# A causal mask moved from matrix products to the row maximum, and partial-array products put side by side

## The chip, the cores and the metric

The kernel runs on one core of a Trainium2 chip. Four engines matter here. TensorE multiplies matrices, VectorE (DVE) and ScalarE (ACT) do element work, and SyncE (SP) issues the transfers from the chip's main memory; GpSimd (POOL) computes a few reciprocal square roots. Each engine works through its own queue in order, and waits where an instruction needs something from another engine or from an earlier instruction of its own. The metric is the time of one execution on the device, in microseconds (us).

## The reference

One decoder layer on 256 positions of width 1024. What the change touches is the first of three stages, the block attention; with 256 positions there is one key block, so it is plain causal attention over eight heads of width 64.

```python
def moba_attention(q, k, v):          # 8 heads of 64, one block of 256 keys
    s = jnp.einsum('bhqd,bhkd->bhqk', q, k) * 64 ** -0.5
    s = jnp.where(k_pos[None, :] <= q_pos[:, None], s, NEG_INF)   # causal mask, NEG_INF = -1e30
    p = jax.nn.softmax(s, axis=-1)
    return jnp.einsum('bhqk,bhkd->bhqd', p, v)

proj = rms_norm(x, g_pre_mix) @ w_in  # q, k, v of the attention; q, k, v, gate of the retention
mo = merge_heads(moba_attention(rotary(q), rotary(k), v))
ro = silu(rg) * rms_norm(retention(rotary(rq), rotary(rk), rv))
x = x + rms_norm(jnp.concatenate([mo, ro], -1) @ w_out, g_post_mix)
# then cross-attention (4 heads of 256) into 256 memory rows, then a SwiGLU feed-forward layer
```

The two lines on `s` are condensed here from the reference's code for gathered blocks.

## The kernel before, in words

All weights come in 130 blocks of 128 x 1024 floats. A block is split into a high part (ScalarE copies it to the matrix format, line 135) and a low part (VectorE subtracts, line 136), and each full product is made of three matrix products: high by high, high by low, low by high (lines 856 to 858, and 871 and 874 in the stages that hold the weights still). TensorE runs these full products almost without end; each of lines 856 to 858 covers the whole 128 x 128 array and streams 512 columns.

Between them stand small pieces of work, which are generators that the main loop resumes: a `yield n` puts the next piece n steps later, and the table `WAIT` holds these numbers by name. So the table, and the order in which pieces are spawned, set every engine's queue when the program is built; nothing is decided at run time. A split of a block is put in when no small piece was resumed in a step, or when blocks run low.

The 256 positions are two tiles of 128, t = 0 and t = 1. The names in the profile are these:

- `c_q`, `c_k`, `c_r`: four transposes each (`moba_qk`, line 216, and `ret_qk`, line 325); ScalarE copies the results to `qv` and `kr` (lines 217, 326, 327), from which the score products read.
- `s_m`: scores of the attention (line 275). A head has 64 rows, so a product uses half of the array's rows, and the two halves work as a pair. There are three units: m00 is tile 0 with eight heads of 128 keys; m10 and m11 are tile 1, four heads each of 256 keys. Each unit has two banks of scores and runs through `softmax_unit`: row maximum (line 231), negated and scaled (`nb`, line 235), exponentials with row sums (line 241), reciprocal and product with it (lines 244, 246), eight transposes (`pt_m`, line 254), and their copies `ptT` (ScalarE line 259, VectorE line 261).
- `maskb`, `identb`: the causal mask is added as a matrix product of the identity with the mask into the same bank (line 278), two per unit.
- `rs`, `ra`: scores of the retention (line 339, again 64 rows each) and their product with the decay table on VectorE (line 346); `ro` is the retention's output (lines 357, 360).
- `o_m`: the value products of the attention (line 304), which use 64 of the array's columns; tile 0 and tile 1 each have a stretch.
- `hl` is a split block, `R_mem` a copied row of norms, `rv` and `mv` copied projections, `junk<-memn` the mean squares of the memory rows.

The banks that `accS` hands out are four, used in turn: a new user waits until the engine that read the last one is done with it.

Of the kernel before, what the change touches and what calls it, by code (L numbers as in the profile page):

```python
# [7 lines left out]
F32 = mybir.dt.float32  # L8
F32R = mybir.dt.float32r
BF16 = mybir.dt.bfloat16  # L10
# [12 lines left out]
NQ = 130  # L23

WAIT = {
# [8 lines left out]
}  # L34
WARM = 8

# [6 lines left out]
def tile_hybrid_layer(  # L43
# [39 lines left out]
    def accS(name):  # L83
        return psS.tile([P, 512], F32, tag="S", name=name)
# [8 lines left out]
    xg = cpool.tile([P, 288], F32, tag="xg", name="xg")  # L93
    gp = xg[:, 0:32].rearrange("p (g k) -> p g k", g=4)
    x_sb = cpool.tile([P, 2, D], F32, tag="x", name="x_sb")
    identb = cpool.tile([P, P], BF16, tag="identb", name="identb")
    maskb = cpool.tile([P, P], BF16, tag="maskb", name="maskb")
    junk = cpool.tile([P, D], BF16, tag="junk", name="junk")
    mhalf = cpool.tile([P, 8], F32, tag="mhalf", name="mhalf")
    ident = cst[:, C_ID:C_ID + P]  # L100
# [116 lines left out]
        nc.scalar.activation(T[f"{kind}T"][:, :, tok(t)], c, AF.Copy)  # L217
        emitted.add(f"{kind}{t}")

    def softmax_unit(key, n, keys, scale, fill, row=None, finish=None):  # L220

        hn = n // 2
        s = [accS(f"s_{key}{b}") for b in range(2)]
        yield from fill(s)
        mx = small(f"mx_{key}")
        nb = small(f"nb_{key}")
        sums = small(f"sum_{key}")
        rs = small(f"rs_{key}")
        p = p4.tile([P, D], F32, tag="p4", name=f"p_{key}")
        for b in range(2):  # L230
            nc.vector.reduce_max(out=mx[:, b * hn:(b + 1) * hn], in_=s[b].rearrange("p (h k) -> p h k", h=hn),
                                 axis=AX.X)
        if row is None:
            esc = scale
            nc.vector.tensor_scalar(nb[:, :n], mx[:, :n], -scale, None, op0=ALU.mult)
        else:
            esc = rs[:, 7:8]
            nc.vector.tensor_scalar(esc, row[:, 0:1], scale, None, op0=ALU.mult)
            nc.vector.tensor_scalar(nb[:, :n], mx[:, :n], row[:, 0:1], -scale, op0=ALU.mult, op1=ALU.mult)
        for i in range(n):  # L240
            nc.scalar.activation(p[:, i * keys:(i + 1) * keys], s[i // hn][:, (i % hn) * keys:(i % hn + 1) * keys],
                                 AF.Exp, bias=nb[:, i:i + 1], scale=esc, accum_out=sums[:, i:i + 1])
# [3 lines left out]
        nc.vector.tensor_tensor(out=p3, in0=p3, in1=rs[:, :n, None].to_broadcast([P, n, keys]), op=ALU.mult)  # L246
        yield WAIT[f"nm_{key}"]
        if finish is None:
            pt = pt4.tile([P, 8, P], F32, tag="pt4", name=f"ptT_{key}")
            T[f"pt_{key}"] = pt  # L250
        for b in range(2):
            s2 = accS(f"pt_{key}{b}")
            for j in range(4):
                nc.tensor.transpose(s2[:, j * P:(j + 1) * P], p[:, (4 * b + j) * P:(4 * b + j + 1) * P], ident)  # L254
            src = s2.rearrange("p (j k) -> p j k", j=4)
            if finish is not None:
                finish(b, src)
            elif b == 0:
                nc.scalar.activation(pt[:, 0:4, :], src, AF.Copy)
            else:  # L260
                nc.vector.tensor_copy(pt[:, 4:8, :], src)

    def moba_unit(t, g):
        keys = P * (t + 1)
        n = D // keys
        hn = n // 2

        def fill(s):

            need(f"q{t}", *[f"k{u}" for u in range(t + 1)])  # L270
            for i in range(hn):
                j = g * hn + i
                for e in range(2):
                    rows = slice(64 * e, 64 * e + 64)
                    nc.tensor.matmul(s[e][:, i * keys:(i + 1) * keys], T["qT"][rows, j, tok(t)],  # L275
                                     T["kT"][rows, j, 0:keys], start=(i == 0), stop=False, skip_group_check=True)
            for e in range(2):
                nc.tensor.matmul(s[e].rearrange("p (h k) -> p h k", h=hn)[:, :, keys - P:keys], identb,
                                 maskb[:, None, :].to_broadcast([P, hn, P]), start=False, stop=True,
                                 skip_group_check=True)  # L280
            yield 0

        return softmax_unit(f"m{t}{g}", n, keys, 0.125, fill)

    def moba_units():
        yield from moba_unit(0, 0)
        yield WAIT["u1"]
        yield from moba_unit(1, 0)
        yield WAIT["u2"]
        yield from moba_unit(1, 1)  # L290

    def moba_pv(t):
        need("mv0", f"mv{t}")
        v = T["mv"]
        c = accC(f"o_m{t}")
        for j in range(4):
            for kb in range(t + 1):
                for e in range(2):
                    h = 2 * j + e
                    if t == 0:  # L300
                        rhs = T["pt_m00"][:, 4 * e + j, :]
                    else:
                        rhs = T[f"pt_m1{j // 2}"][:, 2 * (2 * e + j % 2) + kb, :]
                    nc.tensor.matmul(c[64 * e:64 * e + 64, j, :], v[:, kb, h * 64:h * 64 + 64], rhs,  # L304
                                     start=(kb == 0), stop=(kb == t), skip_group_check=True)
        split4("mixT", 0, t, c)
        yield 0


# [142 lines left out]
        return [pt4.tile([P, 4, 256], F32R, tag="pt4", name=f"{name}{i}") for i in range(2)]  # L452

    def cross_unit(t):
        def fill(s):
            qh, ql, kh, kl = T["cqh"], T["cql"], T["ckh"], T["ckl"]
            for h in range(4):
                for kk in range(2):
                    k = 2 * h + kk
                    tri(s[h // 2][:, (h % 2) * 256:(h % 2 + 1) * 256],  # L460
                        (qh[:, k, tok(t)], ql[k // 4][:, k % 4, tok(t)]), (kh[:, k, :], kl[:, k, :]), kk == 0, kk == 1)
                if h == 1:
                    yield WAIT[f"sc_c{t}"]
            emitted.add(f"cs{t}")
# [9 lines left out]
        return softmax_unit(f"c{t}", 4, 256, 0.0625, fill, rstd[f"x1{t}"], finish)  # L474

    def cross_pv(hp):
        need(f"pc0{hp}", f"pc1{hp}")
# [59 lines left out]
    def in_done(chunk, t, acc):  # L537
        if chunk == 0:
            spawn(moba_qk("q", t, acc), WAIT["mq"])
        elif chunk == 1:  # L540
            spawn(moba_qk("k", t, acc))
            if t == 1:
                spawn(moba_units(), WAIT["u0"])
        elif chunk == 2:
            spawn(ret_qk(t, acc))
            if t == 1:
                spawn(ret_scores(), WAIT["rsc"])
        elif chunk == 3:
            evac(T["rv"][:, t, :], acc, rstd[f"x{t}"][:, 0:1])
            emitted.add(f"rv{t}")  # L550
            if t == 1:
                spawn(ret_out(0), WAIT["ro0"])
                spawn(ret_out(1), WAIT["ro1"])
        elif chunk == 4:
            spawn(ret_gate(t, acc))
        else:
            evac(T["mv"][:, t, :], acc, rstd[f"x{t}"][:, 0:1])
            emitted.add(f"mv{t}")
            spawn(moba_pv(t), WAIT[f"pv{t}"])

    def out_done(c, t, acc):
        post_half("mix", t, c, acc)
# [214 lines left out]
        yield 0  # L777

    def x_stats():
        nc.vector.tensor_copy(identb, ident)  # L780
        nc.vector.tensor_copy(maskb, cst[:, C_MASK:C_MASK + P])
        for t in range(2):
            ss = small(f"ss_x{t}")
            mean_square(ss[:, 0:1], x_sb[:, t, :], D)
# [233 lines left out]
```

## Time and profile before

| what | value |
|---|---|
| median of 3 runs | 408.96 us (408.43 to 409.5) |
| the profiled execution: time, span | 409.01 us, 407.2 us |
| granted TensorE clock, mean | 0.996 |
| TensorE busy | 399.3 us (98% of the span) |
| VectorE busy | 283.2 us (70%) |
| ScalarE busy | 238.4 us (59%) |
| read from main memory | 74.76 MB, 186 GB/s over the span |

The span runs from the first to the last instruction on the core; the execution's own time is 1.8 us longer. In a timeline row the first number is the start, the second the duration, then come engine, line and operation, the tile written and the tiles read, the shapes, and the count of instructions merged; a bracket at the end gives idle time before the row and what ended it. A product of plain 32-bit operands stands as two instructions. Products overlap their ends, so the distance from one start to the next is what a product costs TensorE, not its duration; the same holds for VectorE and ScalarE in a lesser degree.

### The profile page before, as it was taken

What the parts mean: (1) busy time and instruction counts of PE and PEld (TensorE: products, weight loads), DVE (VectorE), ACT (ScalarE), POOL (GpSimd) and SP (SyncE); (2) the same over time, 40 slices, a digit from 0 to 9 for tenths busy, and PEclk for the clock granted to TensorE, in tenths of its full rate; (3) what the DMA queues carried; (4) which work ended last, traced back from release to release, by engine and by line L of the source; (5) the groups of instructions that cost most, each with busy time, mean ns of one, the idle gap of its engine ahead of it and who ended that gap; (6) DMA issues with size and microseconds to landing.
All of it is one profiled execution on the core that took longest, in us unless ns stands there. A gap on an engine that the chain in (4) does not pass through costs nothing.

```text
span 407.2 us, 5752 instructions
## 1 busy us (share of the span) xinstructions
PE 399.3 (98%) x2114; PEld 336.4 (83%) x2114; DVE 283.2 (70%) x456; ACT 238.4 (59%) x438; POOL 11.9 (3%) x21
## 2 busy tenths in 40 slices
PE   8999999999999999999999999999999999999993
PEld 4888787888888889888888888888888888888882
DVE  4885975765989966578359567794884685776632
ACT  5887785935776764686248566564563663564411
POOL 0010100100010000000010100000000000000000
PEclk9999999999999999999999999999999999999998
DMA  7998654475656566147206765675466468355001
GB/s 278 412 358 264 227 200 155 151 260 173 204 194 205 173 206 190 34 175 258 105 8 205 266 233 168 183 221 215 155 192 225 156 172 291 109 159 199 0 29 74
DMA packets 21627, 76.17 MB, mean 187 GB/s; under 512 B 2400, under 2 KB 2656, under 8 KB 21600
## 3 DMA queue, kind: packets, MB, share of 16 engines
q1 hardware_dynamic: 21456, 75.56, 55.2%
q8 instruction: 16, 0.26, 0.3%
q10 hardware_dynamic: 144, 0.26, 0.2%
q14 instruction: 11, 0.09, 0.1%
HBM read 74.76 MB, written 1.05 MB: 186 GB/s over the span
## 4 chain that ended last, share of the span: by engine, by line
PE 95%; issue 2%; DMA 1%; ACT 1%; DVE 0%; SPq 0%; DVEq 0%; POOLq 0%; POOL 0%
PE acc L871 23%; PE acc L874 12%; PE acc L856 12%; PE acc L858 12%; PE acc L857 12%; PE down L892 4%; PE down L893 4%; PE down L894 4%; PE acc L843 2%; DMA xr<-in_gx_dram 1%; PE s_m L275 1%; PE o_m L304 1%; PE pt_m L254 1%; PE ro L357 0%; PE s_c L444 0%
## 5 line engine op out<-in xcount | busy, mean ns | idle before, releaser
L136 DVE TENSOR_TENSOR hl<-raw,hl 128x1024 fp32r<-128x1024 f32 (+1 forms) x132 | 154.6, 1197 | 38.7 <-ACT hl L135 38.2
L135 ACT ACTIVATE hl<-raw 128x1024 fp32r<-128x1024 f32 (+1 forms) x132 | 132.9, 1037 | 9.4 <-DMA raw<-in_weights_dram 7.0
L871 PE MATMUL acc<-x2T,hl 128*128 128x512 f32 x288 | 72.5, 392 | 0.0
L871 PEld LDWEIGHTS acc<-x2T,hl 128*128 128x128 f32 x288 | 52.0, 189 | 9.4
L874 PEld LDWEIGHTS acc<-x2T,hl 128*128 128x128 f32 x288 | 39.3, 190 | 2.8
L874 PE MATMUL acc<-x2T,hl 128*128 128x256 f32 x288 | 40.1, 282 | 0.0
L892 PE MATMUL down<-hl,fT 128*128 128x512 f32 x88 | 34.3, 390 | 0.0
L893 PE MATMUL down<-hl,fT 128*128 128x512 f32 x88 | 34.3, 390 | 0.0
L894 PE MATMUL down<-hl,fT 128*128 128x512 f32 x88 | 34.2, 389 | 0.0
L856 PE MATMUL acc<-hl,xT 128*128 128x512 f32 x80 | 32.7, 409 | 0.0
L858 PE MATMUL acc<-hl,xT 128*128 128x512 f32 x80 | 31.3, 391 | 0.0
L857 PE MATMUL acc<-hl,xT 128*128 128x512 f32 x80 | 31.2, 390 | 0.0
L516 ACT ACTIVATE sg<-sg 128x256 f32<-128x256 f32 x18 | 7.5, 417 | 21.3 <-DVE sg L514 21.3
L894 PEld LDWEIGHTS down<-hl,fT 128*128 128x128 f32 x88 | 16.5, 188 | 3.5
L892 PEld LDWEIGHTS down<-hl,fT 128*128 128x128 f32 x88 | 16.5, 188 | 3.3
L893 PEld LDWEIGHTS down<-hl,fT 128*128 128x128 f32 x88 | 16.5, 188 | 3.3
L511 ACT ACTIVATE sg<-acc 128x256 f32<-128x256 f32 x18 | 6.8, 378 | 19.3 <-PE acc L874 19.2
L858 PEld LDWEIGHTS acc<-hl,xT 128*128 128x128 f32 x80 | 15.0, 188 | 3.3
L856 PEld LDWEIGHTS acc<-hl,xT 128*128 128x128 f32 x80 | 15.1, 188 | 3.1 <-issue 0.3
L447 ACT ACTIVATE fT<-sg 128x256 fp32r<-128x256 f32 x18 | 7.5, 419 | 17.0 <-DVE sg L528 16.9
L857 PEld LDWEIGHTS acc<-hl,xT 128*128 128x128 f32 x80 | 15.1, 188 | 2.7
L513 DVE TENSOR_TENSOR sg<-acc,sg 128x256 f32<-128x256 f32 x18 | 7.6, 421 | 12.7 <-ACT sg L511 12.7
(209 smaller groups left out, 695.0 us busy)
## 6 DMA issues: line engine op xcount, KB each, us to landing
raw<-in_weights_dram SPq DMA_DIRECT2D x129, 512.0 KB, 4.4
gpost<-in_gpost_dram SPq DMA_DIRECT2D x3, 512.0 KB, 5.6
x_sb<-in_x_dram SPq DMA_DIRECT2D x2, 512.0 KB, 6.9
memn<-in_mem_dram SPq DMA_DIRECT2D x2, 512.0 KB, 6.7
mr<-in_memT_dram SPq DMA_DIRECT2D x2, 512.0 KB, 5.3
out_dram<-x_sb SPq DMA_DIRECT2D x4, 256.0 KB, 2.0
xr<-in_gx_dram SPq DMA_DIRECT2D x1, 512.0 KB, 8.3
cst<-in_consts_dram SPq DMA_DIRECT2D x1, 512.0 KB, 7.9
```

The lines of the kernel that those rows point to most:

```text
L135: nc.scalar.activation(h[:, 0, n], raw[:, n], AF.Copy)
L136: nc.vector.tensor_tensor(out=h[:, 1, n], in0=raw[:, n], in1=h[:, 0, n].bitcast(F32), op=ALU.subtract)
L513: nc.vector.tensor_tensor(out=sg, in0=acc[:, 0:256], in1=sg, op=ALU.add)
L843: nc.tensor.matmul(accs[(c, t)], T["xT"][:, hx, 2 * kp + kk, tok(t)], h[:, hw, :], start=begin, stop=False)
L856: nc.tensor.matmul(acc, xh, h[:, 0, kk, :], start=(first and kk == 0), stop=False)
L857: nc.tensor.matmul(acc, xh, h[:, 1, kk, :], start=False, stop=False)
L858: nc.tensor.matmul(acc, xl, h[:, 0, kk, :], start=False, stop=(last and kk == 1))
L871: nc.tensor.matmul(acc, hls[q][:, 0, k * P:(k + 1) * P], T[f"{st}_k"][:, k, :], start=(k == 0), stop=False, skip_group_check=True)
L874: nc.tensor.matmul(acc[:, 0:256], hls[q][:, 1, k * P:(k + 1) * P], T[st][:, 0, k, :], start=False, stop=(k == 7), skip_group_check=True)
L892: nc.tensor.matmul(acc, fh, wh, start=first, stop=False, skip_group_check=True)
L893: nc.tensor.matmul(acc, fh, wl, start=False, stop=False, skip_group_check=True)
L894: nc.tensor.matmul(acc, fl, wh, start=False, stop=last, skip_group_check=True)
```

## The change

The mask is no longer a matrix product. VectorE adds it with an instruction that adds two operands, writes the sum back into the score bank and keeps the row maximum (`tensor_tensor_reduce`), one per head; the maximum over both heads' banks (`reduce_max`) stays for the cross-attention. A table of 256 columns, zeros and then the mask, takes the place of the two 16-bit tiles.

The score products of m00 and m10 are issued together, and those of m11 directly ahead of the first retention scores, instead of each with its own unit. The value products of both tiles are issued together, into two of the four score banks instead of the single bank that `accC` hands out. The table of waits is another one in nearly every entry, and two names are new: a wait after the maximum (`mx_`) and one halfway through the exponentials (`eh_`).

```diff
 WAIT = {
-    "cpb0": 1, "cpb1": 0, "cpv0": 7, "cpv1": 3, "cu0": 1, "cu1": 4, "ex_c0": 0, "ex_c1": 1, "ex_m00": 0,
+    "cpb0": 1, "cpb1": 3, "cpv0": 7, "cpv1": 1, "cu0": 0, "cu1": 2, "eh_c0": 2, "eh_c1": 1, "eh_m00": 2,
...
-    identb = cpool.tile([P, P], BF16, tag="identb", name="identb")
-    maskb = cpool.tile([P, P], BF16, tag="maskb", name="maskb")
+    maskz = cpool.tile([P, 256], F32, tag="maskz", name="maskz")
...
-    def softmax_unit(key, n, keys, scale, fill, row=None, finish=None):
+    def softmax_unit(key, n, keys, scale, s, row=None, finish=None):
...
-        for b in range(2):
-            nc.vector.reduce_max(out=mx[:, b * hn:(b + 1) * hn], in_=s[b].rearrange("p (h k) -> p h k", h=hn),
-                                 axis=AX.X)
+        if row is None:
+
+            for i in range(n):
+                a = s[i // hn][:, (i % hn) * keys:(i % hn + 1) * keys]
+                nc.vector.tensor_tensor_reduce(out=a, in0=a, in1=maskz[:, 256 - keys:256], scale=1.0, scalar=-3.0e38,
+                                               op0=ALU.add, op1=ALU.max, accum_out=mx[:, i:i + 1])
+        else:
...
+        yield WAIT[f"mx_{key}"]
         for i in range(n):
+            if 2 * i == n:
+                yield WAIT[f"eh_{key}"]
...
-            for e in range(2):
-                nc.tensor.matmul(s[e].rearrange("p (h k) -> p h k", h=hn)[:, :, keys - P:keys], identb,
-                                 maskb[:, None, :].to_broadcast([P, hn, P]), start=False, stop=True,
-                                 skip_group_check=True)
...
     def moba_units():
-        yield from moba_unit(0, 0)
+
+        units = [moba_scores(0, 0), moba_scores(1, 0)]
+        spawn(units[0])
         yield WAIT["u1"]
-        yield from moba_unit(1, 0)
+        spawn(units[1])
         yield WAIT["u2"]
-        yield from moba_unit(1, 1)
+        last = moba_scores(1, 1)
+        scores = ret_scores()
+        wait = next(scores)
+        spawn(scores, wait)
+        yield from last
...
-    def moba_pv(t):
-        need("mv0", f"mv{t}")
+    def moba_pv():
+        need("mv0", "mv1")
         v = T["mv"]
-        c = accC(f"o_m{t}")
...
+        banks = [accS("o_m0").rearrange("p (j m) -> p j m", j=4), accS("o_m1").rearrange("p (j m) -> p j m", j=4)]
+        for t in range(2):
+            c = banks[t]
```

The built queues differ in many places; three of them are shown, names with the program's buffer numbers. First VectorE, from the scores of m00 to the product with the reciprocal, before:

```order
L231 TENSOR_REDUCE mx_m_423<-s_m_411 128x4
L231 TENSOR_REDUCE mx_m_423<-s_m_412 128x4
L235 TENSOR_SCALAR nb_m_424<-mx_m_423 128x8
L244 RECIPROCAL rs_m_426<-sum_m_425 128x8
L246 TENSOR_TENSOR p_m_427<-p_m_427,rs_m_426 128x1024
```

And in the change, with the waits shown, the first bank's last head, the second bank, and what follows:

```order
L233 ISA s_m000_489,mx_m00_536<-s_m000_489,maskz_96 128x128 [waits DVE_49]
L233 ISA mx_m00_536 128x1
L233 ISA s_m001_490,mx_m00_536<-s_m001_490,maskz_96 128x128 [waits PE_49]
L233 ISA mx_m00_536 128x1
L233 ISA s_m001_490,mx_m00_536<-s_m001_490,maskz_96 128x128 [waits DVE_49]
```

The two reductions have become eight instructions on 128 columns, each followed by one that writes the maximum; from the second head of a bank on, each waits for VectorE's own instruction before it.

Second ScalarE, up to the copies of `c_r` of tile 1 into `kr`, which the retention's scores read; before:

```order
L241 ACTIVATE p_m_582,sum_m_580<-s_m_571,nb_m_579 128x256 x2
L135 ACTIVATE hl_592<-raw_397 128x1024
L178 ACTIVATE R_mem<-c_R_mem 128x256
L135 ACTIVATE hl_614<-raw_455 128x1024
L170 ACTIVATE rv<-acc_526,r_x_282 128x512
L135 ACTIVATE hl_632<-raw_474 128x1024
L170 ACTIVATE rv<-acc_550,r_x_288 128x512
L135 ACTIVATE hl_644<-raw_524 128x1024
L326 ACTIVATE kr<-c_r_656 128x2x128
L327 ACTIVATE kr<-c_r_656 128x2x128
```

And in the change:

```order
L136 ACTIVATE hl_560<-raw_370 128x1024
L179 ACTIVATE R_mem<-c_R_mem 128x256
L250 ACTIVATE p_m_540,sum_m_538<-s_m_490,nb_m_537 128x128 x4
L136 ACTIVATE hl_598<-raw_400 128x1024
L171 ACTIVATE rv<-acc_476,r_x_264 128x512
L250 ACTIVATE p_m_586,sum_m_584<-s_m_499,nb_m_583 128x256 x2
L250 ACTIVATE p_m_586,sum_m_584<-s_m_500,nb_m_583 128x256 x2
L136 ACTIVATE hl_622<-raw_431 128x1024
L171 ACTIVATE rv<-acc_522,r_x_270 128x512
L136 ACTIVATE hl_634<-raw_474 128x1024
L268 ACTIVATE ptT_m_646<-pt_m_647 128x512
L335 ACTIVATE kr<-c_r_666 128x2x128
```

Ahead of the copies into `kr` now stand the second half of m00's exponentials, all of m10's, and the copy of m00's transposes; before, m00's unit was over long ahead of this place.

Third TensorE, at the scores of m11 and the first of the retention; before:

```order
L275 MATMUL s_m_701<-kr,qv 128x256
L278 LDWEIGHTS identb
L278 MATMUL s_m_700<-maskb,identb 128x2x128
L278 LDWEIGHTS identb
L278 MATMUL s_m_701<-maskb,identb 128x2x128
L339 MATMUL rs_720<-kr 128x256
L339 MATMUL rs_721<-kr 128x256
```

And in the change, with what follows up to the transposes of m10:

```order
L282 MATMUL s_m_684<-kr,qv 128x256
L282 MATMUL s_m_685<-kr,qv 128x256
L348 MATMUL rs_690<-kr 128x256
L348 MATMUL rs_691<-kr 128x256
L348 MATMUL rs_690<-kr 128x256
L348 MATMUL rs_691<-kr 128x256
L864 MATMUL acc_659<-hl_560,xT 128x512
```

The mask's products are gone and the two kinds of scores follow each other. At 60 full products ahead of this place stand, also side by side, the transposes `c_q` of tile 1 and the scores of m00 and m10; before, m00's scores stood some 100 full products ahead of the retention's, and m10's 54.

More of the change, by code (lines that the diff above doesn't have):

```diff
@@ L261, in softmax_unit, with moba_scores @@
                 nc.vector.tensor_copy(pt[:, 4:8, :], src)
-    def moba_unit(t, g):
+    def moba_scores(t, g):
         keys = P * (t + 1)
[L265 to L272, printed above, removed]
-                for e in range(2):
-                    rows = slice(64 * e, 64 * e + 64)
-                    nc.tensor.matmul(s[e][:, i * keys:(i + 1) * keys], T["qT"][rows, j, tok(t)],
-                                     T["kT"][rows, j, 0:keys], start=(i == 0), stop=False, skip_group_check=True)
-            for e in range(2):
-                nc.tensor.matmul(s[e].rearrange("p (h k) -> p h k", h=hn)[:, :, keys - P:keys], identb,
-                                 maskb[:, None, :].to_broadcast([P, hn, P]), start=False, stop=True,
-                                 skip_group_check=True)
-            yield 0
-        return softmax_unit(f"m{t}{g}", n, keys, 0.125, fill)
+        hn = D // keys // 2
+        need(f"q{t}", *[f"k{u}" for u in range(t + 1)])
+        s = [accS(f"s_m{t}{g}{b}") for b in range(2)]
+        for i in range(hn):
+            j = g * hn + i
+            for e in range(2):
+                rows = slice(64 * e, 64 * e + 64)
+                nc.tensor.matmul(s[e][:, i * keys:(i + 1) * keys], T["qT"][rows, j, tok(t)],
+                                 T["kT"][rows, j, 0:keys], start=(i == 0), stop=(i == hn - 1), skip_group_check=True)
+        return softmax_unit(f"m{t}{g}", 2 * hn, keys, 0.125, s)
@@ new lines, in moba_units @@
+        scores = ret_scores()
[4 more added lines that the diff above has]
+        need("mv0", "mv1")
+        v = T["mv"]
+        banks = [accS("o_m0").rearrange("p (j m) -> p j m", j=4), accS("o_m1").rearrange("p (j m) -> p j m", j=4)]
+        for t in range(2):
+            c = banks[t]
+            for j in range(4):
+                for kb in range(t + 1):
+                    for e in range(2):
+                        h = 2 * j + e
+                        if t == 0:
+                            rhs = T["pt_m00"][:, 4 * e + j, :]
+                        else:
+                            rhs = T[f"pt_m1{j // 2}"][:, 2 * (2 * e + j % 2) + kb, :]
+                        nc.tensor.matmul(c[64 * e:64 * e + 64, j, :], v[:, kb, h * 64:h * 64 + 64], rhs,
+                                         start=(kb == 0), stop=(kb == t), skip_group_check=True)
+            split4("mixT", 0, t, c)
@@ L454, in cross_unit @@
     def cross_unit(t):
[L455 to L464, printed above, removed]
+        s = [accS(f"s_c{t}{b}") for b in range(2)]
+        qh, ql, kh, kl = T["cqh"], T["cql"], T["ckh"], T["ckl"]
+        for h in range(4):
+            for kk in range(2):
+                k = 2 * h + kk
+                tri(s[h // 2][:, (h % 2) * 256:(h % 2 + 1) * 256],
+                    (qh[:, k, tok(t)], ql[k // 4][:, k % 4, tok(t)]), (kh[:, k, :], kl[:, k, :]), kk == 0, kk == 1)
+            if h == 1:
+                yield WAIT[f"sc_c{t}"]
+        emitted.add(f"cs{t}")
         def finish(b, src):
@@ L472, in finish @@
             emitted.add(f"pc{t}{b}")
-        return softmax_unit(f"c{t}", 4, 256, 0.0625, fill, rstd[f"x1{t}"], finish)
+        yield from softmax_unit(f"c{t}", 4, 256, 0.0625, s, rstd[f"x1{t}"], finish)
     def cross_pv(hp):
@@ L779, in x_stats @@
     def x_stats():
-        nc.vector.tensor_copy(identb, ident)
-        nc.vector.tensor_copy(maskb, cst[:, C_MASK:C_MASK + P])
+        nc.vector.memset(maskz[:, 0:P], 0.0)
+        nc.vector.tensor_copy(maskz[:, P:256], cst[:, C_MASK:C_MASK + P])
         for t in range(2):
```

21 lines of the change are left out of this document (5 added, 16 removed), and 16 rows, old and new, of the table WAIT.

## The prediction

> **What bounds the kernel now.** First the page's head and busy times, then the list of what TensorE waited for.
>
> ```profile
> span 407.2 us, 5752 instructions
> PE 399.3 (98%) x2114; PEld 336.4 (83%) x2114; DVE 283.2 (70%) x456; ACT 238.4 (59%) x438; POOL 11.9 (3%) x21
> ```
>
> ```profile
> PE acc L843 <- ACT hl L806: 0.6, 1, 0.6
> ```
>
> TensorE is busy 98% of the span. The list of its waits has one other entry, 1.2 us ahead of the warm-up products; the one shown lies among the first weight blocks. After that its stream never stops, so the time is the sum of what each product costs, start to start, and a change can gain only by taking products or switches out, and lose only by making TensorE wait. VectorE (70%) and ScalarE (59%) bound nothing on average; whether they do so in one stage must be read there. Third, the timeline of TensorE at the places of the change (start, duration, engine, line, operation):
>
> ```profile
> 32.77 0.60 PE L216 MATMUL c_q<-cst,nat_q 128*128 128x128 f32 x4
> 33.29 1.16 PE L275 MATMUL s_m<-kr,qv 64*128 64x128 f32 x16
> 34.39 0.60 PE L278 MATMUL s_m<-maskb,identb 128*128 128x512 bf16 x2
> ...
> 35.30 0.40 PE L858 MATMUL acc<-hl,xT 128*128 128x512 f32 x1
> ...
> 47.73 1.13 PE L275 MATMUL s_m<-kr,qv 64*128 64x256 f32 x8
> 48.80 0.39 PE L278 MATMUL s_m<-maskb,identb 128*128 128x256 bf16 x2
> ...
> 49.49 0.39 PE L858 MATMUL acc<-hl,xT 128*128 128x512 f32 x1
> ...
> 51.76 0.38 PE L177 MATMUL c_R_mem<-cst,r_mem 128*128 128x128 f32 x2
> ...
> 64.36 1.13 PE L339 MATMUL rs<-kr 64*128 64x256 f32 x8
> 65.42 0.50 PE L856 MATMUL acc<-hl,xT 128*128 128x512 f32 x1
> ...
> 65.99 0.40 PE L858 MATMUL acc<-hl,xT 128*128 128x512 f32 x1
> ...
> 87.57 0.39 PE L858 MATMUL acc<-hl,mixT 128*128 128x512 f32 x1
> 87.89 1.09 PE L304 MATMUL o_m<-ptT_m,qv 128*64 128x128 f32 x16
> ...
> 89.48 0.39 PE L858 MATMUL acc<-hl,mixT 128*128 128x512 f32 x1
> ...
> 92.44 0.40 PE L858 MATMUL acc<-hl,mixT 128*128 128x512 f32 x1
> 92.76 1.97 PE L304 MATMUL o_m<-ptT_m,qv 128*64 128x128 f32 x32
> ...
> 95.23 0.39 PE L858 MATMUL acc<-hl,mixT 128*128 128x512 f32 x1
> ```
>
> A full product costs 0.227 us: ten of them lie between 49.49 and 51.76. Everything else is measured against that.
>
> **What is removed from TensorE.** The value products give the price of a switch. Stretch one, from the last full product ahead of it (87.57) to the third one counted from there (89.48), is 1.91 us, less three products at 0.227: 1.23. Stretch two, with 32 rows instead of 16 (92.44 to 95.23), is 2.79, less 0.68: 2.11. So 16 further rows cost 0.88, and going into a stretch of partial products and out again costs 1.23 - 0.88 = 0.35. The change has three such switches fewer: m10's scores follow m00's, the retention's follow m11's, and tile 1's value products follow tile 0's. I take 0.35 for each, 1.05 in all.
>
> The mask: in m00, from its first row to the second full product behind (34.39 to 35.30) 0.91, where two full products behind scores without a mask take 0.57 (65.42 to 65.99); the mask costs 0.34. In m10 it is 0.69 (48.80 to 49.49) against 0.57, so 0.12, and m11 has the same shape: 0.12. Together 0.58. **Saved on TensorE: 1.05 + 0.58 = 1.6 us.** All other pieces that change their place on TensorE (transposes, `c_k`, `c_r`, `ro`) cost the same elsewhere.
>
> **What is added to VectorE.** Sixteen add-and-maximum instructions with sixteen small ones that write the maximum, for six reductions; two copies of a mask become a copy and a fill. The trace has no such instruction. Its nearest rows:
>
> ```profile
> L527 DVE TENSOR_TENSOR sg<-acc,sg 128x256 f32<-128x256 f32 x18 | 7.6, 420 | 4.0 <-ACT sg L524 4.0
> L430 DVE SCALAR_TENSOR_TENSOR x1T<-xt_mix,xg,x1T 128x128 fp32r<-128x128 f32 x16 | 4.4, 344 | 0.0
> ...
> ```
>
> ```profile
> 34.81 1.29 DVE L231 TENSOR_REDUCE mx_m<-s_m 128x4 f32<-128x512 f32 x2 [0.43 <-PE s_m L278]
> 36.14 0.17 DVE L235 TENSOR_SCALAR nb_m<-mx_m 128x8 f32<-128x8 f32 x1
> ...
> 39.58 1.22 DVE L246 TENSOR_TENSOR p_m<-p_m,rs_m 128x1024 f32<-128x1024 f32 x1
> ...
> 43.33 0.42 DVE L318 TENSOR_TENSOR rt_r<-nat_r,cst 128x256 f32<-128x256 f32 x1
> 43.78 0.69 DVE L320 TENSOR_TENSOR nat_r<-nat_r,cst 128x512 f32<-128x512 f32 x1
> ...
> 60.57 1.23 DVE L136 TENSOR_TENSOR hl<-raw,hl 128x1024 fp32r<-128x1024 f32 x1 [0.27 <-ACT hl L135]
> 61.71 0.69 DVE L261 COPY ptT_m<-pt_m 128x512 f32<-128x512 f32 x1
> ```
>
> A two-operand instruction from a score-like bank takes 0.42 us on 256 columns, and 512 columns take 0.69 (the rows at 43.78 and 61.71), so 128 take 0.42 - 0.13 = 0.285. The next instruction starts 0.08 before its end when nothing binds them (60.57 + 1.23 against 61.71). When it waits for the one before on its own engine it starts 0.03 after that end (43.33 + 0.42 against 43.78), and from the second head of a bank on the queue's rows show this wait. The maximum's write I price at the smallest row here, 0.17 (36.14). A pair then costs 0.285 - 0.08 + 0.17 + 0.03 = 0.40 on 128 columns and 0.54 on 256. So m00's group takes 8 x 0.40 = 3.2 us where the reductions take 1.33 (34.81 to 36.14), and m10's and m11's take 4 x 0.54 = 2.16 each. Low bound: the write costs nothing beyond its neighbours, 0.24 and 0.37. High bound: the three-operand row, 0.344 on 128 columns, and 0.20 for the write, 0.49 and 0.63. I take the middle, because the instruction has two tensor operands as in L527 and the wait is in the queue.
>
> [...]
>
> **What hides it, and for how long.** Before, m00's unit was over long before m10's began. Now both softmax units must pass between the joined scores and the retention's scores `rs`, because the copies of `c_r` into `kr` that `rs` reads stand behind both on ScalarE. TensorE's way there, from the start of `c_q` of tile 1: 0.52 for the transposes (32.77 to 33.29) and 1.0 for m00 (33.29 to 34.39, less 0.1 for the exit); then from m10's first row to the first `rs` row. Before that was 16.63 (47.73 to 64.36) with 54 full products; now it is 60, so 6 x 0.227 = 1.36 more, and four more transposes, 0.45 (0.52 without the switch), less two masks and a part of a switch, 0.5. Sum 0.52 + 1.0 + 17.9 = **19.4 us**.
>
> The other way, on ScalarE and VectorE, in the new order of their queues, at the durations of these rows (ScalarE):
>
> ```profile
> 33.40 0.60 ACT L217 ACTIVATE qv<-c_q 128x512 f32<-128x512 f32 x1 [0.28 <-PE c_q L216]
> 36.40 0.37 ACT L241 ACTIVATE p_m<-s_m,nb_m 128x128 f32<-128x128 f32 x1 [2.40 <-DVE nb_m L235]
> ...
> 44.80 1.06 ACT L153 ACTIVATE junk<-memn 128x1024 bf16<-128x1024 f32 x1
> ...
> 47.04 1.05 ACT L135 ACTIVATE hl<-raw 128x1024 fp32r<-128x1024 f32 x1
> ...
> 48.25 0.37 ACT L327 ACTIVATE kr<-c_r 128x256 f32<-128x256 f32 x1
> ...
> 51.88 0.47 ACT L241 ACTIVATE p_m<-s_m,nb_m 128x256 f32<-128x256 f32 x1 [3.26 <-DVE nb_m L235]
> ...
> 53.70 1.07 ACT L135 ACTIVATE hl<-raw 128x1024 fp32r<-128x1024 f32 x1
> 54.65 0.39 ACT L178 ACTIVATE R_mem<-c_R_mem 128x256 f32<-128x256 f32 x1
> 54.91 1.08 ACT L135 ACTIVATE hl<-raw 128x1024 fp32r<-128x1024 f32 x1
> 55.86 0.71 ACT L170 ACTIVATE rv<-acc,r_x 128x512 f32<-128x512 f32 x1
> 56.43 1.09 ACT L135 ACTIVATE hl<-raw 128x1024 fp32r<-128x1024 f32 x1
> ```
>
> - From `c_q` to its copy 0.63 (32.77 to 33.40), the copy 0.57 (as 55.86 to 56.43): 1.2.
> - Two mean squares of the memory, now directly behind it, 2.24 (44.80 to 47.04): 3.4. A split, 1.08 on ScalarE until VectorE may subtract, 1.14 there (60.57 to 61.71): 5.7. Only here do the maxima of m00 start, though their scores stand ready since about 2.
> - m00's maxima 3.2, to the exponentials 0.26 (36.14 to 36.40), eight exponentials and the reciprocal 3.18 (36.40 to 39.58), between their halves a split 0.95 and `R_mem` 0.26 (53.70 to 54.91), the normalization 1.14: 14.7.
> - m10's maxima 2.16, 0.26, exponentials 1.82 (51.88 to 53.70): 18.9. A split 0.95, `rv` 0.57, a split 0.95, the copy of m00's transposes 0.57, the first copy into `kr` 0.37 (48.25) and 0.05 to wake TensorE: **22.35 us**.
>
> So the first `rs` product is late by 22.35 - 19.4 = 2.95. The second needs the bank that VectorE empties with its copy of m00's transposes, which stands behind the second of those splits: ScalarE starts that at 20.4, VectorE at 21.5, done 22.6, the copy 0.69 (61.71) and 0.05, 23.35: 0.95 later still, 3.9. Next is `ro` of tile 0, which needs the bank that VectorE empties with its copy of m10's transposes, and this stands behind m11's maxima. TensorE reaches it at 23.35 + 0.95 for `rs` + 12 x 0.227 + 0.9 for eight transposes + 0.1 = 28.0. VectorE has the two decay products from 24.7 (1.29, as the reductions' row of equal width), the maxima 2.16, 0.1, and the copy 0.69: 28.9. Late by 0.9. Sum of waits **4.8 us**. Nothing gives it back: TensorE's stream after it is full, and what waits behind the waiting product are the full products themselves.
>
> **Sum.** -1.6 + 4.8 = +3.2 on 409.0, the profiled execution's own time (its span is 1.8 less, and it stands 0.05 above the median): **412.2 us**. With the high prices the two chains grow by 8 x 0.09 + 4 x 0.09 = 1.1 and 0.36: 413.7. With the low ones they shrink by 1.96 and 0.68: 409.6. The forecast's own range is 410.3 to 414.
>
> **The rivals.**
> 1. *The cover holds*: TensorE never waits, as before, and only the saved products count: 409.0 - 1.6 = 407.4. For it: the lateness is a difference between two sums of about 20 us, and ScalarE was priced with its work ahead done at the old pace. Against it: even maxima as cheap as the old reductions (1.33 and 1.28) leave about 0.2 + 0.95 of waiting, because the VectorE copy behind the split remains. It decides where the first `rs` row follows m11's scores with no gap. Chance 0.18.
> 2. *A cheap pair*: the maximum's write hides wholly behind its neighbours, low bound, 409.6, no change that could be told. For it: 0.08 of overlap is seen between VectorE's instructions. Against: the waits in the queue. Chance 0.17.
> 3. *Two cycles a column*: the new instruction runs at half the pace, 0.135 more on 128 columns and 0.27 on 256 (0.69 - 0.42), so 1.08 + 1.08 ahead of `rs` and 1.08 ahead of `ro`: 412.2 + 3.2 = 415.4. For it: the trace has no instruction that combines two operands and reduces. Against: every two-operand row here runs at one. Chance 0.12. [...]
> 4. *The value products wait too*: tile 1's stand about 2.3 us behind m11's transposes (four transposes 0.45, 16 rows 1.0, 16 rows 0.88), and their copies, 0.6 to 0.7, can stand behind one split of 1.1 on VectorE. That is covered; a second split ahead would cost one more 1.1: 413.3. Chance 0.08.
>
> **How the numbers follow.** The forecast has 0.45. A measurement of this kernel tells 0.3% (1.2 us) from no change, so faster is below 407.7 and slower above 410.2. Faster is rival 1, 0.18; same is rival 2, 0.17; slower are the forecast and rivals 3 and 4, 0.65. The range that leaves 2 in 10 out reaches down to rival 1 and up past the high bound, without rival 3: 407.2 to 414.6.
>
> **What would show it.** In the new profile TensorE should have about 1.6 us less between starts at the four joined places, no row of `maskb`, and waits at three: before the first and the second `rs` product (about 3.9 us together, some of it already before m00's transposes), and before `ro` (0.9). VectorE's add-and-maximum rows should be near 0.285 and 0.42 long, and a group from first row to `nb` 3.2 and 2.2. If no wait stands at `rs`, the chain was wrong; if the groups are long and there is still no wait, TensorE's 19.4 was; if VectorE's rows are far from these, the price was.

## The result, and the profile after

| | before | changed |
|---|---|---|
| median (5 executions each) | 409.01 us | 413.17 us |
| range | 408.43 to 409.64 | 412.4 to 416.0 |
| ratio, 95% interval | | 1.0113 [1.0095, 1.0131] |
| profiled execution: time, span | 409.01, 407.2 | 413.17, 411.4 |
| its mean granted TensorE clock | 0.996 | 0.991 |

The change makes the kernel 1.1% slower. The forecast was 412.2 us, its own range 410.3 to 414. First the head of the new page, and the new list of TensorE's waits (us in total, times, longest), without the two that stand ahead of 9 us as before:

```profile
span 411.4 us, 5763 instructions
PE 400.2 (97%) x2108; PEld 338.2 (82%) x2108; DVE 287.7 (70%) x482; ACT 236.5 (57%) x438; POOL 11.0 (3%) x21
```

```profile
PE rs L348 <- ACT kr L335: 1.9, 1, 1.9
...
PE pt_m L263 <- ACT rv L171: 0.9, 1, 0.9
...
PE rs L348 <- DVE ptT_m L270: 0.5, 1, 0.5
```

Three waits, where there was none: before m00's transposes, before the first retention scores, and before their second pair. The first is put down to the copy `rv`, which ended at 56.52; the product with the reciprocals, which the transposes read, ended at 56.49, so VectorE's chain binds there as well. Next TensorE's timeline from m11's scores on:

```profile
60.85 1.13 PE L282 MATMUL s_m<-kr,qv 64*128 64x256 f32 x8
63.85 0.70 PE L348 MATMUL rs<-kr 64*128 64x256 f32 x2 [1.86 <-ACT kr L335]
65.03 1.13 PE L348 MATMUL rs<-kr 64*128 64x256 f32 x6 [0.48 <-DVE ptT_m L270]
66.09 0.53 PE L864 MATMUL acc<-hl,xT 128*128 128x512 f32 x1
66.42 0.62 PE L865 MATMUL acc<-hl,xT 128*128 128x512 f32 x1
66.84 0.63 PE L866 MATMUL acc<-hl,xT 128*128 128x512 f32 x1
...
68.12 0.63 PE L866 MATMUL acc<-hl,xT 128*128 128x512 f32 x1
```

The last rows hold what the predicted sum did not have: full products start 0.42 us apart instead of 0.227. The windows show why. Their columns are the stretch, its length, busy time (and instructions) of TensorE, its weight loads, VectorE, ScalarE, GpSimd, then the granted TensorE clock, the DMA share and GB/s:

```profile
60.00:65.00 5.00, 2.68 (x14) 1.38 (x13) 4.27 (x5) 5.00 (x11) 0.00 (x0) 1.00 0.43 138
65.00:70.00 5.00, 4.97 (x21) 3.98 (x21) 4.36 (x12) 0.34 (x2) 0.00 (x0) 0.66 0.81 281
70.00:75.00 5.00, 5.00 (x32) 4.18 (x31) 2.09 (x3) 4.45 (x15) 0.56 (x1) 1.00 0.12 13
```

Cut finer, the clock stands at 0.50 from 66.4 to 69.8, a stretch of 3.4 us that begins 2.6 us after the first `rs` product (63.85) and 1.4 us after the second pair (65.03), when TensorE had gone back to work.

Third the new instructions of VectorE, grouped by line and shape (busy us, mean ns | idle before), and their sequence:

```profile
L233 DVE CUSTOM_DVE_ANT_0 s_m<-s_m,maskz 128x256 f32<-128x256 f32 x8 | 3.3, 438 | 0.1
L233 DVE CUSTOM_DVE_ANT_0 s_m<-s_m,maskz 128x128 f32<-128x128 f32 x8 | 2.3, 302 | 0.2
L233 DVE DVE_READ_ACCUMULATOR2_ANT mx_m<- 128x1 f32 x16 | 2.3, 141 | 0.0
```

```profile
46.54 1.23 DVE L137 TENSOR_TENSOR hl<-raw,hl 128x1024 fp32r<-128x1024 f32 x1 [0.80 <-ACT hl L136]
47.68 0.29 DVE L233 CUSTOM_DVE_ANT_0 s_m<-s_m,maskz 128x128 f32<-128x128 f32 x1
47.89 0.14 DVE L233 DVE_READ_ACCUMULATOR2_ANT mx_m<- 128x1 f32 x1
48.06 0.30 DVE L233 CUSTOM_DVE_ANT_0 s_m<-s_m,maskz 128x128 f32<-128x128 f32 x1
...
50.66 0.17 DVE L241 TENSOR_SCALAR nb_m<-mx_m 128x8 f32<-128x8 f32 x1
```

A pair costs 0.38 start to start here (47.68 to 48.06), and m00's group 2.98 (47.68 to 50.66). The other ends of the chain are these rows: the transposes it starts from, the first mean square of the memory rows, m10's first maximum and its `nb`, and the split behind m10's exponentials:

```profile
41.28 0.60 PE L217 MATMUL c_q<-cst,nat_q 128*128 128x128 f32 x4
...
43.13 1.06 ACT L154 ACTIVATE junk<-memn 128x1024 bf16<-128x1024 f32 x1 [0.43 <-DMA memn<-in_mem_dram]
...
56.41 0.42 DVE L233 CUSTOM_DVE_ANT_0 s_m<-s_m,maskz 128x256 f32<-128x256 f32 x1
...
58.43 0.17 DVE L241 TENSOR_SCALAR nb_m<-mx_m 128x4 f32<-128x4 f32 x1
...
60.45 1.07 ACT L136 ACTIVATE hl<-raw 128x1024 fp32r<-128x1024 f32 x1
```

**Where the time went.** The cost of each stretch of partial products is taken as in the prediction (start to start, less its full products), in the profiled executions:

| stretch on TensorE | before | changed | difference |
|---|---|---|---|
| `c_q` of tile 1, m00, m10 | 2.08 + 1.41 | 2.65 | -0.84 |
| m00's transposes | 0.89 | 2.02 | +1.13, a wait |
| m11, first `rs` | 2.65 | 5.63 | +2.98: 0.5 saved, 3.3 of waits, 0.2 of half clock |
| full products and m10's transposes behind it | 0.68 + 0.89 | 1.28 + 1.72 | +1.43, half clock |
| m11's transposes, one `c_ro`, value products | 4.69 | 4.29 | -0.39 |

Saved 1.74, waited 4.42, lost at half clock 1.62, and the first blocks were through 0.13 earlier (the first row of line 856, now 864, at 16.74 instead of 16.87): +4.17. The profiled times differ by 4.16. The 0.5 saved in the third row comes from the runs below, where the stretch has no wait (2.15). The list gives the three waits 3.3 us in all; counted start to start they cost 4.4.

### The profile page after: what moved, and what is told of

Read it like the earlier page. It is cut to its first block, busy times and chain, and to the rows that moved or that the text cites. A ratio compares the mean times of both kernels' runs of the same rounds, so it can differ in the third digit from the quotient of the medians.

```text
span 411.4 us, 5763 instructions
## 1 busy us (share of the span) xinstructions
PE 400.2 (97%) x2108; PEld 338.2 (82%) x2108; DVE 287.7 (70%) x482; ACT 236.5 (57%) x438; POOL 11.0 (3%) x21
## 3 DMA queue, kind: packets, MB, share of 16 engines
HBM read 74.76 MB, written 1.05 MB: 184 GB/s over the span
## 4 chain that ended last, share of the span: by engine, by line
PE 86%; DMA 3%; DVE 3%; ACT 3%; issue 3%; SPq 0%; DVEq 0%; POOLq 0%; POOL 0%; ACTq 0%
PE acc L879 23%; PE acc L882 12%; PE acc L864 10%; PE acc L865 10%; PE acc L866 10%; PE down L901 4%; PE down L900 4%; PE down L902 4%; PE acc L851 2%; DMA memn<-in_mem_dram 2%; DMA raw<-in_weights_dram 1%; ACT p_m L250 1%; DVE hl L137 1%; DVE s_m L233 1%; ACT hl L136 1%
## 5 line engine op out<-in xcount | busy, mean ns | idle before, releaser
L879 PE MATMUL acc<-memT,hl 128*128 128x512 f32 x64 | 16.4, 396 | 0.0
L879 PE MATMUL acc<-x1T,hl 128*128 128x512 f32 x64 | 16.0, 392 | 0.0
```

The costliest lines, as they stand in the source:

```text
L879: nc.tensor.matmul(acc, hls[q][:, 0, k * P:(k + 1) * P], T[f"{st}_k"][:, k, :], start=(k == 0), stop=False, skip_group_check=True)
```

## The experiments

**1. The mask alone goes back to TensorE.** Joins, order and waits of the change are kept.

```diff
-            for i in range(n):
...
-                nc.vector.tensor_tensor_reduce(out=a, in0=a, in1=maskz[:, 256 - keys:256], ...)
...
+        for b in range(2):
+            nc.vector.reduce_max(out=mx[:, b * hn:(b + 1) * hn], ...)
...
+        for e in range(2):
+            nc.tensor.matmul(s[e].rearrange(...)[:, :, keys - P:keys], identb, maskb[...], start=False, stop=True)
```

> The changed kernel, with the mask as matrix products again and the two reductions per unit in place of the sixteen add-and-maximum pairs; joins and table of waits stay. Theory (the lateness is the length of one chain on ScalarE and VectorE): the maxima of m00 fall from 2.98 to 1.33 us and those of m10 from 2.02 to 1.28, so the chain is 2.4 shorter; TensorE's way there is 0.46 longer (two masks). The 0.94 + 1.86 us of waits before m00's transposes and the first rs product go, at most 0.5 stays before the second, no stretch at half clock follows, and the time is 409.0 - 0.7 (two switches) + up to 0.5: 408.3 to 408.9. Rival 1 (the order of the queues alone makes the lateness, not the price of the maxima): waits of over 2 us stay at rs, time over 411. Rival 2 (the half clock comes from something else in the new order): a stretch at 0.5 is there without a wait, time about 410.

Measured: 408.80 us beside 408.78 for the kernel before, ratio 1.0002 [0.9993, 1.0011], clock 0.995 to 0.999 in all eleven executions. No wait of TensorE is listed behind 2 us, and there is no stretch at half clock. So the theory holds and both rivals are out: with the reductions' price, the order of the change is late by little. It is not wholly free, as these rows show:

```profile
61.46 1.46 PE L346 MATMUL rs<-kr 64*128 64x256 f32 x8
62.85 0.50 PE L862 MATMUL acc<-hl,xT 128*128 128x512 f32 x1
```

The eight products of `rs` take 1.39 here where they took 1.06 (64.36 to 65.42 in the kernel before), so some 0.3 is lost among them, within the 0.5 that was expected there. This takes back most of what the joined value products save, 0.40 (4.29 beside 4.69). The joined scores save next to nothing: `c_q`, m00 and m10 cost 3.46 (3.49 before). With mask products between the two units, joining them saves no switch.

**2. The mask alone goes to VectorE, in the kernel before.**

```diff
-            for e in range(2):
-                nc.tensor.matmul(s[e].rearrange(...)[:, :, keys - P:keys], identb, maskb[...], ...)
...
-            nc.vector.reduce_max(out=mx[:, b * hn:(b + 1) * hn], ...)
...
+                nc.vector.tensor_tensor_reduce(out=a, in0=a, in1=maskz[:, 256 - keys:256], ...)
```

> The kernel before, with only the mask changed: the add-and-maximum pairs on VectorE, no mask products; order, joins and table as before. Theory (the pairs are only dear where the cover was taken away by the joined scores): TensorE loses 0.58 us of masks and one switch of 0.35 (m11's scores now stand next to the retention's); m00's longer maxima lie under slack, those of m10 and m11 (0.74 each more) may let TensorE wait up to 1 us. Time 408.1 to 409.2. Rival (the pairs alone make VectorE late, whatever the order): waits of 2 us or more, as in the changed kernel, and 411 or more.

Measured: 409.97 us, ratio 1.0031 [1.0020, 1.0043], above the theory's 409.2 and far below the rival's 411. The three stretches with a mask became cheaper by 0.34, 0.13 and 0.51 (2.08 to 1.74, 1.41 to 1.27, 2.65 to 2.15): 0.98 in all. New waits took it back:

```profile
PE c_r L327 <- DVE nat_r L323: 0.6, 1, 0.6
PE rs L341 <- DVE ra L348: 0.3, 1, 0.3
PE pt_m L260 <- DVE p_m L252: 0.3, 1, 0.3
```

Counted start to start, the three stretches that hold these waits cost 0.76, 0.84 and 0.44 more, 2.04 in all. My expectation that m00's maxima lie under slack was wrong. Before, the product with the reciprocals ended at 40.8 (39.58 + 1.22) and m00's transposes began at 42.15, 1.3 later; the longer group takes 1.65 more, and TensorE comes 0.34 sooner. So in the old order too the pairs use up more time than VectorE has there, though half as much as in the new one.

**3. Pauses made by hand in the kernel before**, to see whether standing still brings the half clock. A chain of GpSimd powers (4, 6 or 9) starts with VectorE's copy of m10's transposes and ends in one extra transpose ahead of the first `rs`:

```diff
+            if kb == 0:
+                w = T["pt_m10"][:, 4, 0:1]
+                for _ in range(4):
+                    z = small("pause")
+                    nc.gpsimd.tensor_tensor(out=z[:, 0:1], in0=rstd["x0"][:, 0:1], in1=w, op=ALU.pow)
+                    w = z[:, 0:1]
+                nc.tensor.transpose(s[0][:, 0:P], w.to_broadcast([P, P]), ident)
```

> The kernel before, with a pause made by hand: a chain of 4 small GpSimd powers, started by VectorE's copy of m10's transposes (ends at 62.4 us), feeds one extra transpose ahead of the retention's first scores (64.3 us). Nothing else waits for it. At 0.55 to 1.0 us a power the pause is 0.5 to 2.3 us. Theory (TensorE's granted clock falls to a half for some us because TensorE stood still): a stretch at 0.5 follows the pause in some executions, the mean clock falls below 0.996, and those executions cost 1 to 2 us more than the pause. Rival (the half clock in the changed kernel came from load at this place, not from standing still): granted clock as before, time 409.0 + pause + 0.1.

> The pause made by hand again, with 6 powers. The two measured pauses (4 powers 0.6 us, 9 powers 3.8 us) give 0.64 a power, so 1.9 us, as long as the longest wait in the changed kernel. Theory (a pause of this length can bring one stretch of 3.4 us at half clock, by where it falls): 409.0 + 1.9 + 0.5 for starting again = 411.2 without the stretch, 412.9 with it, both seen or one of them. Rival (it takes a longer pause, and the changed kernel's half clock came from its three waits following each other): always about 411.2 and granted clock as before.

> As the short pause, with 9 powers: a pause of 3.2 to 7.2 us. Theory: a stretch at half clock follows in every execution, about as long as in the changed kernel (3.3 us, 1.7 lost) or longer, time 409.0 + pause + 1.5 to 2. Rival: no stretch at half clock, 409.0 + pause + 0.1.

The waits of the three kernels, short, middle and long:

```profile
PE rs L342 <- POOL pause L340: 0.6, 1, 0.6
```

```profile
PE rs L342 <- POOL pause L340: 1.9, 1, 1.9
```

```profile
PE rs L342 <- POOL pause L340: 3.8, 1, 3.8
```

| pause | time (before) | mean clock of the executions |
|---|---|---|
| 0.6 us | 409.89 (408.78) | 0.996 to 0.999 in six |
| 1.9 us | 412.34 (409.03) | 0.992 or 0.993 in three (412.2 to 412.8), 0.996 in one (411.09) |
| 3.8 us | 415.24 (408.78) | 0.989 in four |

The windows behind the long pause:

```profile
64.00:66.00 2.00, 0.00 (x0) 0.00 (x0) 1.25 (x3) 0.62 (x3) 1.76 (x4) 1.00 0.46 186
66.00:68.00 2.00, 0.38 (x1) 0.18 (x1) 0.00 (x0) 2.00 (x7) 1.41 (x3) 0.51 0.00 0
68.00:70.00 2.00, 2.00 (x9) 1.19 (x8) 0.00 (x0) 0.25 (x1) 0.00 (x0) 0.50 0.00 0
70.00:72.00 2.00, 2.00 (x7) 1.58 (x6) 1.86 (x3) 0.00 (x0) 0.00 (x0) 0.50 0.00 0
72.00:74.00 2.00, 2.00 (x15) 1.23 (x14) 0.92 (x3) 0.00 (x0) 0.00 (x0) 0.78 0.35 37
```

The kernel before has no half clock at this place; with a pause of 1.9 us it has one in three executions of four, and with 3.8 us in all four. One execution of each kernel was traced, and for the others this is read from the mean clock. Without any stretch the mean is 0.995 to 0.999. In the traced execution of the kernel before, its 0.996 comes from the end: the last product starts at 400.7, and the clock is at 0.50 from 403.7 to 407.2, which takes 0.004 from the mean. The theory for the short pause was missed: the traced execution with 0.6 us has no stretch, and the six lie within 0.8 us, with a mean clock as before. The DMA share is 0.00 where the clock is low (66 to 72 behind the long pause, 68 to 70 behind the middle one), so load from transfers in the stretch is not the cause. The stretch ran from 67.5 to 70.9 behind the middle pause, 3.4 us as in the changed kernel, and from 66.0 to 72.9 behind the long one, twice 3.4. Both cases that were expected of the middle pause came: 411.09 with the clock kept, 412.5 in the median of the others, so the half clock cost 1.4.

**4. The mean squares of the memory rows left out of the change**, a term of 2.24 us in the predicted chain that the change had only moved.

```diff
-            mean_square(ss[:, 0:1], mn[t], D)
+            nc.vector.memset(ss[:, 0:1], 1.0)
```

> The changed kernel without the two mean squares of the memory rows on ScalarE (they are set to one, so the norm of the memory is left out of the computation; two small fills on VectorE stand in their place). Theory (the chain as predicted, where the mean squares stand on the path with 2.24 us and, in the changed kernel's trace, 0.43 of waiting for the memory rows): the maxima of m00 start 2.7 earlier, the three waits fall from 3.28 to 0.6, no half clock, time 409.0 - 1.7 + 0.6 + 0.2 = about 408. Rival (VectorE's own queue stands close behind: the rotation of the retention's rows and two splits of 1.2 each end there about 1.1 us before the maxima start now): the maxima start only 1.1 earlier, 2.2 us of waits stay, time 409 to 411 by whether a stretch at half clock follows.

Measured: 411.93 us beside 409.03, ratio 1.0080 [1.0055, 1.0104]. VectorE where m00's maxima begin, and TensorE's waits:

```profile
45.46 1.23 DVE L137 TENSOR_TENSOR hl<-raw,hl 128x1024 fp32r<-128x1024 f32 x1
46.60 0.29 DVE L233 CUSTOM_DVE_ANT_0 s_m<-s_m,maskz 128x128 f32<-128x128 f32 x1
```

```profile
PE rs L348 <- ACT kr L335: 1.7, 1, 1.7
...
PE rs L348 <- DVE ptT_m L270: 0.5, 1, 0.5
```

The maxima begin at 46.60, 1.08 earlier than in the change, and 2.2 us of waits remain. The split ahead of them now shows no idle time before it: VectorE's own work, which the predicted chain leaves out at this place, stood 1.08 behind ScalarE's. So the rival holds for the start and the waits. Its time, 409 to 411, was too low: the 2.2 us listed cost 3.2 start to start (m11 and the first `rs` take 5.39), and in the profiled execution a stretch at half clock, from 65.5 to 68.9, costs 1.6 more (the full products and m10's transposes behind `rs` take 1.28 + 1.86 beside 0.68 + 0.89).

**5. The change with other waits**, and the same with the mask back on TensorE as in run 1. Of the table 22 numbers differ from the change (the expectation says 20), and nothing else does; only these entries are shown.

```diff
-    "eh_m00": 2, "eh_m11": 4, "ex_m10": 0, "ex_m11": 5, "gate0": 1, "mrow": 3, "mst": 4, "mx_m00": 0, "mx_m10": 3,
-    "nm_m00": 5, "ro0": 5, "ro1": 8, "rope_k0": 9, "rope_k1": 3, "rope_q0": 3, "rope_q1": 4, "rope_r0": 3,
-    "rope_r1": 10, "rs": 2, "u0": 9, "u1": 2, "xs": 10,
+    "eh_m00": 1, "eh_m11": 5, "ex_m10": 2, "ex_m11": 4, "gate0": 2, "mrow": 4, "mst": 5, "mx_m00": 1, "mx_m10": 6,
+    "nm_m00": 4, "ro0": 6, "ro1": 6, "rope_k0": 8, "rope_k1": 6, "rope_q0": 4, "rope_q1": 5, "rope_r0": 4,
+    "rope_r1": 9, "rs": 1, "u0": 10, "u1": 1, "xs": 9,
```

> The changed kernel with 20 other numbers in the table of waits and nothing else: c_q of tile 1 and the joined scores of m00 and m10 come one step later and more work stands between the maxima, the exponentials and the retention's scores. Theory (the pairs and the joins cost TensorE nothing once VectorE and ScalarE have time): no wait of TensorE behind 10 us, no stretch at half clock, and the saving as measured piece by piece, 0.98 for the masks (0.34, 0.13, 0.51), 0.36 for the joined scores and 0.40 for the joined value products, 1.74 in all: 407.0 beside 408.8 for the kernel before. Rival (the pairs cost more than VectorE's place allows in any order): some wait of 1 us or more stays, 408.5 or more.

> The same table of waits, with the mask as matrix products again and the two reductions per unit. Theory (what moving the mask is worth where nothing waits): 0.34 + 0.13 + 0.51 = 1.0 us more than the retimed kernel, and the joined scores save almost nothing with mask products between them (0.03 in the first run of this kind): 408.0 to 408.4, no waits. Rival (the mask products are hidden anyway): the same time as the retimed kernel, 407.0.

Measured: the retimed change 407.35 us beside 409.03, ratio 0.9958 [0.9946, 0.9971]; with the mask back 408.80, 0.9993 [0.9984, 1.0002]. The retimed change is faster than the kernel before and the change, as its theory had it; with the mask back the time cannot be told from the kernel before. TensorE in the two, at m11 and the first `rs`:

```profile
59.90 1.13 PE L282 MATMUL s_m<-kr,qv 64*128 64x256 f32 x8
60.86 1.03 PE L348 MATMUL rs<-kr 64*128 64x256 f32 x8
```

```profile
61.25 1.14 PE L276 MATMUL s_m<-kr,qv 64*128 64x256 f32 x8
62.32 0.39 PE L279 MATMUL s_m<-maskb,identb 128*128 128x256 bf16 x2
62.64 1.13 PE L346 MATMUL rs<-kr 64*128 64x256 f32 x8
```

The only wait left in the first is the one ahead of the warm-up products; m11's eight rows and the retention's follow each other 0.96 apart, with the mask the starts are 1.39 apart. The saving is 1.68 where the pieces sum to 1.74. Between the two kernels lie 1.45, and not the 1.0 that I had written, so the second is above the 408.0 to 408.4 expected: I had left out that the joined scores lose their 0.36 too when mask products come between them (3.47 against 2.61, and 2.65 against 2.15, 1.37 together). So moving the mask is what makes the joined scores worth anything, and the rest, 0.4, is the joined value products.

**6. The change with TensorE kept busy in its wait.**

```diff
-        for i in range(hn):
+        again = 3 if g else 1
+        for i in [i for _ in range(again) for i in range(hn)]:
```

> The changed kernel with TensorE kept busy in its longest wait: the scores of m11 are computed three times over in place of once (the same values into the same banks, 16 products of 0.12 us more, 1.96 us, where TensorE stands still for 1.86 before the retention's first scores). VectorE and ScalarE have the same work. Theory (the half clock comes from standing still, and apart from it the forecast's chain sets the time): no stretch at half clock in most executions, granted clock 0.995 to 0.999, the wait before the first rs product nearly gone, and the wait before ro that the forecast had (0.9) shows with 0.5 to 0.9, because TensorE is no longer slowed ahead of it; time 411.9 to 412.5, near the one execution of the changed kernel at 0.997 (412.4) and below its median of 413.2. Rival (the half clock belongs to the place or its load): still a stretch at half clock, 413 to 414. Second rival (more work costs more): 413.2 + 2.

Measured: 412.35 us beside 409.07 (412.01 to 412.52), ratio 1.0077 [1.0063, 1.0090], clock 0.995 to 0.999 in all five executions. TensorE's waits and clock:

```profile
PE rs L349 <- DVE ptT_m L270: 0.5, 1, 0.5
PE pt_m L263 <- ACT rv L171: 0.3, 1, 0.3
PE ro L367 <- DVE ptT_m L270: 0.2, 1, 0.2
```

```profile
60.00:65.00 5.00, 4.37 (x32) 2.94 (x32) 4.39 (x6) 4.85 (x9) 0.00 (x0) 1.00 0.47 134
65.00:70.00 5.00, 4.86 (x26) 3.54 (x26) 4.83 (x13) 0.49 (x3) 0.00 (x0) 1.00 0.80 285
```

Sixteen products more, and 0.8 us less than the change's median. (That the wait before m00's transposes is 0.6 shorter here is little gain: in this execution TensorE reached `c_q` at 41.75, 0.47 later.) The load in the second window is that of the change (0.80 and 285 GB/s beside 0.81 and 281), and the clock is 1.00 instead of 0.66: it was the standing still. Both rivals are out. Now `ro` waits as the forecast had it, though less: 0.2 by the list, and 0.5 start to start, since its stretch costs 2.25 beside 1.74 in the change.

## Why the prediction was right, and where it was not

**The sum.** Forecast -1.6 + 4.8 = +3.2; measured -1.7 + 4.4 + 1.6 less 0.1 at the start = +4.2. The direction, the mechanism and the places around `rs` held. The size is short by a term that the sum did not have, the 1.6 at half clock. That the waits come near 4.8 is partly luck: 3.9 were forecast around `rs` and cost 4.4, and the 0.9 before `ro` did not come.

**The saving** was 1.05 for three switches and 0.58 for the masks. The masks measure 0.34, 0.13 and 0.51, the last with m11's switch in it (0.12 + 0.35 predicted); the joined scores 0.36 (3.01 without masks and unjoined in run 2, 2.65 joined); the value products 0.39. Each is within 0.05.

**The pair** was priced 0.40 and 0.54; the groups took 2.98 and 2.02 where 3.2 and 2.16 stood. The instruction itself is 0.30 and 0.44, near the two-operand row (0.285 and 0.42), so rival 3 is out: its half pace would be 0.42 and 0.69 (the rows give 1.05 ns a column; the length of a cycle was not shown). The two lengths lie 0.136 apart for 128 columns, where the two-operand rows have 0.135 (284 ns at line 211 and 419 at line 316 in the kernel before). The write of the maximum, 0.14, hides only a little, since a pair costs 0.38 where the low bound was 0.24, so rival 2 is out. By an estimate from the two lengths (302 and 438 ns), 0.17 of the 0.30 does not grow with the columns, and m00's eight instructions pay it eight times.

**The chain** against the change's trace, from `c_q` at 41.28 to the first `rs` at 63.85:

| step | predicted | measured |
|---|---|---|
| to the start of m00's maxima | 5.7 | 6.40 |
| m00's maxima | 3.2 | 2.98 |
| exponentials to the end of the product with the reciprocals | 5.8 | 5.75 |
| m10's maxima | 2.16 | 2.02 |
| its exponentials | 2.1 | 2.02 |
| to the first `rs` | 3.45 | 3.40 |
| sum (the rows of the forecast are rounded) | 22.35 | 22.57 |

TensorE's way, 19.4, comes out as 19.40: m11 begins 19.57 after `c_q` (60.85), less the 1.13 that m00's transposes lost, plus 0.96. So the first `rs` is late by 3.17 (predicted 2.95), part of it already before m00's transposes, as the prediction said. The second pair comes 1.18 behind the first, where two products of this shape take 0.24 without a wait (m11's eight 0.96 in the retimed kernel): 0.94 (predicted 0.95). Together this is 4.1; the other 0.3 of the 4.4 lies in the six products behind the second wait, which take 1.06 (65.03 to 66.09) where six of the eight in the retimed kernel take 0.72. No run shows why. Rival 1 is out.

In the first row, 0.43 of the 0.7 that was missing is a wait for the memory rows, which the forecast did not have. ScalarE's mean squares, priced with 2.24, were the bound as forecast, but by less than their length: run 4 took them away and the start moved by 1.08. VectorE's rotations and splits, which I had not laid out for this place, are the next bound, and it is luck that this omission cost nothing.

**The wait before `ro`** (0.9) did not come in the change, since TensorE had been slowed ahead of it; in run 6, at full clock, it costs 0.5. The mechanism was right, the size was too large.

**What was missing** is the step "nothing gives it back: TensorE's stream after it is full", which took TensorE's pace after a wait to be the pace before. In the profiled execution 1.6 us went there. Without them it would be 411.6, and 412.1 with the 0.5 before `ro` that run 6 shows; the one execution of the change with the clock at 0.997 took 412.4, and run 6 412.35. So without the half clock the forecast of 412.2 comes out about right. More cannot be said from single executions, since those of the kernel before alone spread over 1.2 us and another one of the change, at 0.991, took 412.65. The executions at 0.987 and 0.988 took 416.0 and 414.4; the long pause, with twice 3.4 us at half clock, has 0.989, so more than one stretch may have come there too. No trace of them exists, and this stays open. Rival 4 (the value products wait) is out: their stretch costs 4.29 in the change and in the retimed kernel.

## What to carry to other kernels

Work that was moved from a full engine (TensorE, 98% busy) to a half-empty one (VectorE, 70%) was paid in the change at the place where the half-empty engine has its chain: 4.4 us of waits beside 1.74 saved. So lay out both queues between two fixed points and subtract, as was done here; and lay out every engine of the chain, not only the one that seems to bind. With TensorE's stream as the bound, these waits cost that and brought a stretch at half clock behind them, 1.6 us more in the profiled execution; if a wait cannot be removed, harmless products in it can cost less than standing still, as in run 6 (412.35 us beside the change's 413.17). A change that is late by a few us in one place is not yet refuted: with the waits re-chosen the same change gained 0.4%, and its joined scores gained only together with the moved mask.

## What the runs showed of the hardware

In the kernel before, the granted TensorE clock fell to 0.50 after a pause of 1.9 us (three executions of four) or 3.8 us (four of four), and in none of six after 0.6 us; one execution of each was traced, the others are read from their mean clock. In the traced ones it stayed there for 3.4 us behind the middle pause (67.5 to 70.9), as in the change (66.4 to 69.8) and in run 4 (65.5 to 68.9), and for 6.9 behind the long one (66.0 to 72.9). It fell when TensorE was already at work again, 2.6 us later in the change and 1.1 us later behind the middle pause; in the long pause it fell while TensorE still stood, after 2.2 us. The same pause of 1.9 us brought it in three executions and not in the fourth.

A wait cost the stream more than the list of waits says, since the list counts from the end of the last product and the stream from start to start. Behind the first two `rs` products of the change 0.48 is listed and 0.94 lost, because these two last 0.70 by their rows where the next would have started after 0.24. In the middle pause the difference is small: 1.88 is listed and 1.95 lost (64.14 to 66.41, less the 0.32 that the mask's products take there in the kernel before, 64.04 to 64.36), and the extra transpose costs 0.26 more (66.41 to 66.67).
